# Hybrid decoder trunk: value projection by Strassen blocks with input sums made twice and products in another order

## Chip, cores and metric

One core of one Trainium2 chip runs the whole kernel. The metric is the device time of one execution in microseconds; a profile gives the span from the first to the last instruction, and a little lies around it.

## What is computed

Two residual layers on x of 512 tokens by 2048 columns, float32. The change lies in the second one:

```
def odd_layer(x, ln, w_in, w_out):
    h = rmsnorm(x, ln).astype(x.dtype)
    cq, ck, cv, cg = jnp.split(h @ w_in, 4, axis=-1)      # w_in: 2048 x 8192
    ...
    oc = stick_breaking_attention(heads(cq), heads(ck), heads(cv))
    y = (oc * jax.nn.silu(cg.astype(jnp.float32))).astype(x.dtype) @ w_out
    return x + y
```

The stage in question is `cv`, h (512 x 2048) times the value columns of w_in (2048 x 2048).

## The kernel before

All products run on TensorE (PE) in float32r. Each operand is carried as two parts, hi (a rounded copy made on ScalarE, ACT) and lo (the rest, a subtraction on VectorE, DVE); a product is three matmuls, hi x hi, lo x hi and hi x lo. `split` (line 160) makes the pair. Weights lie in DRAM in the order of use. `plan` lists that order as items, `chunk_pieces` cuts items into transfers, and `pump` fetches and splits them ahead of `take`, three jobs ahead at most, since the pools of hi and lo weights (`wp`) have three buffers. PE's instructions stand in program order. Those of the other engines are ordered by a scheduler by priority, and each engine then works strictly in the order that it was given; a helper `urgent` raises the priority.

The first layer ends with `out_proj`; as each of its 16 column blocks is finished, `finish_even` writes it to DRAM (x1), splits it into h2 and adds its square to a running sum (on GpSimd, POOL). Then comes the value projection (lines 983 to 1018), and after it the q, k and gate projections of 16 heads with attention between them, and the last output projection.

The value projection is 512 x 2048 by 2048 x 2048. `V_ORDER` cuts the 2048 columns into two halves g of 1024 and the 2048 rows into two halves kh, so there are four blocks (g, kh) of 1024 by 1024. Each block takes seven products in place of eight, by Strassen's scheme in Winograd's form. A product is a 256-token half by 512 rows (four chunks of 128) by 512 columns: 24 matmuls of 128 x 512, taken as two jobs of 12. Four products take sums of input quarters (s1 to s4, made by `block_operands` per kh: for each of four pairs of chunks two loads from x1, two scalings on ACT, two sums on POOL, two on DVE and two splits) and four take sums of weight quarters (t1 to t4):

```
G: t3 = 22 - 12 (L220), t1 = 12 - 11 (L221), written over 12
V: t2 = t3 + 11 (L223), written over 11
G: t4 = 21 - t2 (L224), written over 21
```

Here G is POOL and V is DVE. Weight quarters lie in a pool of 19 buffers (x) and, for quarter 11, in three raw buffers of the weights. The blocks come in the order (0,0), (0,1), (1,1), (1,0), so kh changes twice and the input sums are made three times: kh = 0 in the call at n == 11 of `finish_even`, kh = 1 before the second block, kh = 0 again before the fourth. The products come in the order 11, 12, s2, s1, s3, s4, 22, with the weights 11, 21, t2 (in 11), t1 (in 12), t3, 22, t4 (in 21). A result is copied out of PSUM by ACT (L1013) the first time and added by DVE (L1015) afterwards; s2 goes on in the PSUM banks that hold product 11, so it waits for the copy. Finished quarters of a half go to DRAM (`vdr`), from where the heads read them later.

Of the kernel before, what the change touches and what calls it, by code (L numbers as in the profile page):

```python
# [38 lines left out]
def plan():  # L39
# [11 lines left out]
    order += [("wo", "S", 2 * D + 2 * S * g, k) for g, k in V_ORDER]  # L51
# [9 lines left out]
V_ORDER = ((0, 0), (0, 1), (1, 1), (1, 0))  # L61
# [6 lines left out]
def chunk_pieces(item):  # L68
# [9 lines left out]
    if kind == "S":  # L78

        c = 8 * item[3]  # L80
        res = [(c, 2, col, 512), (c + 2, 2, col, 512)] + [(c + i, 1, col, 512) for i in range(4, 8)]
        for i in range(4, 8):
            res += [(c + i, 1, col + 512, 512), (c + i - 4, 1, col + 512, 512)]
        return res
# [14 lines left out]
def trunk(ctx, tc, xt, w, lnT, lbT, gnT, qkn, sink, cs, amask, bmask, eye, cmask, out):  # L99
# [92 lines left out]
    sums = [set() for _ in blocks_at]  # L192
    loaded = set()

    def quarter_load(blk, k):
# [8 lines left out]
        if k < 2:  # L204
            for z in range(2):
                quarters[blk]["11", 2 * k + z] = t[:, z * S:(z + 1) * S]
            quarters[blk]["11 pair", k] = t
        else:
            name = ("21", k - 2) if k < 6 else ("12" if k % 2 else "22", (k - 6) // 2)
            quarters[blk][name] = t  # L210

    def quarter_sums(blk, i, late):

        if (i, late) in sums[blk]:
            return
# [10 lines left out]
    OPERANDS = ("11", "21", "11", "12", "t3", "22", "21")  # L226

    def block_ahead(blk, m):
# [3 lines left out]
        for k in range((0, 1, 2, 4, 6, 10, 14)[min(max(m + 1, 0), 6)]):  # L232
            quarter_load(blk, k)
        for i in range(max(0, min(4, 2 * (m - 3)))):
            quarter_sums(blk, i, False)

    def pump(upto):
        while nxt[0] < min(upto, len(jobs)):
# [3 lines left out]
            if isinstance(j, tuple):  # L242
# [4 lines left out]
                if m in (4, 5):  # L247
                    for i in (2 * m - 8, 2 * m - 7):
                        quarter_sums(blk, i, True)
                hi = wp.tile([P, 2 * S], F32R, tag="hi", name=f"bhi{n}")  # L250
                lo = wp.tile([P, 2 * S], F32R, tag="lo", name=f"blo{n}")
                if OPERANDS[m // 2] == "11":
                    split(quarters[blk]["11 pair", m % 2], hi, lo)
                else:
                    for z in range(2):
                        split(quarters[blk][OPERANDS[m // 2], 2 * (m % 2) + z],
# [582 lines left out]
    def block_operands(kh):  # L839


        res = []
        for i in range(4):
            a, b = U(), U()
            for t, c in ((a, 8 * kh + i), (b, 8 * kh + 4 + i)):
                nc.sync.dma_start(out=t, in_=x1[:, c, :])
                A.activation(out=t, in_=t, func=AF.Copy, scale=ln[:, NC + c:NC + c + 1])  # L847
            a1, a2, b1, b2 = a[:, :256], a[:, 256:], b[:, :256], b[:, 256:]
            G.tensor_tensor(out=b2, in0=a2, in1=b2, op=ALU.add)  # L849
            G.tensor_tensor(out=a2, in0=a1, in1=a2, op=ALU.subtract)  # L850
            V.tensor_tensor(out=a1, in0=b2, in1=a1, op=ALU.subtract)  # L851
            V.tensor_tensor(out=b1, in0=b1, in1=a1, op=ALU.subtract)
            both = []
            for t in (a, b):
                hi, lo = U(F32R), U(F32R)
                split(t, hi, lo)
                both.append((hi, lo))
            res.append(both)
        return res

    def block_op(ops, kh, name, i):
        if name[0] == "s":
            src = ops[i][name in ("s1", "s4")]
# [6 lines left out]
    def finish_even(n, t):  # L870
# [8 lines left out]
        if n == 11:  # L879
            ops0.extend(block_operands(0))  # L880

    ops0 = []
# [101 lines left out]
    PRODUCTS = ("11", "12", "s2", "s1", "s3", "s4", "22")  # L984
    res = None
    for blk, (g, kh) in enumerate(V_ORDER):
        if not blk or V_ORDER[blk - 1][1] != kh:
            ops = ops0 if not blk else block_operands(kh)
        last = blk % 2 == 1
        if not last:  # L990
            res = {}
        pairs = [[bank(pp) for _ in range(2)] for _ in range(2)]
        for n, name in enumerate(PRODUCTS):
            if n in (3,):
                pairs[1] = [bank(pp) for _ in range(2)]
            ps = pairs[n % 2]
            new = n in (0, 1, 3)
            for j in range(2):
                hi, lo = take()
                for i in (2 * j, 2 * j + 1):  # L1000
                    a, b = (x[:, (i % 2) * S:(i % 2 + 1) * S] for x in (hi, lo))
                    xh, xl = block_op(ops, kh, name, i)
                    for t in range(2):
                        k = slice(t * P, (t + 1) * P)
                        mm(ps[t], xh[:, k], a, new and not i, False)
# [109 lines left out]
```

## Time and profile before

| | |
|---|---|
| median of 3 runs | 1864.25 us (1862.08 to 1866.0) |
| the profiled execution | 1865.8 us |
| its span | 1864.0 us |
| PE busy | 1817.4 us (98%) |
| DVE, ACT, POOL busy | 1129.2, 834.5, 193.5 us |
| mean granted clock of TensorE | 0.983 |
| DMA | 208.22 MB, 112 GB/s |

[...] Idle time of an engine that is not the bottleneck costs nothing.

### The profile page before, as it was taken

What the parts mean: (1) busy time and instruction counts of PE and PEld (TensorE: products, weight loads), DVE (VectorE), ACT (ScalarE), POOL (GpSimd) and SP (SyncE); (2) the same over time, 40 slices, a digit from 0 to 9 for tenths busy, and PEclk for the clock granted to TensorE, in tenths of its full rate; (3) what the DMA queues carried; (4) which work ended last, traced back from release to release, by engine and by line L of the source; (5) the groups of instructions that cost most, each with busy time, mean ns of one, the idle gap of its engine ahead of it and who ended that gap; (6) DMA issues with size and microseconds to landing.
All of it is one profiled execution on the core that took longest, in us unless ns stands there. A gap on an engine that the chain in (4) does not pass through costs nothing.

```text
span 1864.0 us, 22949 instructions
## 1 busy us (share of the span) xinstructions
PE 1817.4 (98%) x8706; PEld 1507.6 (81%) x8706; DVE 1129.2 (61%) x1707; ACT 834.5 (45%) x1408; POOL 193.5 (10%) x156
## 2 busy tenths in 40 slices
PE   9999999999999999999879799999999999999999
PEld 6988888888888888887758588888888888888887
DVE  7486777866456676346869646555555456555334
ACT  6454645644344453244545435444545354444221
POOL 4012211200000000125534200000000000000000
PEclk9999999999999999999879799999999999999999
DMA  6222232222221236433343242223223323235424
GB/s 228 91 91 90 80 102 91 91 71 79 83 85 69 80 135 228 174 141 130 103 139 116 79 143 88 88 95 114 85 96 109 101 85 108 96 103 181 163 85 152
DMA packets 79166, 208.22 MB, mean 112 GB/s; under 512 B 9296, under 2 KB 9808, under 8 KB 79056
## 3 DMA queue, kind: packets, MB, share of 16 engines
q1 hardware_dynamic: 76752, 202.57, 32.0%
q10 hardware_dynamic: 2304, 4.20, 0.7%
q8 instruction: 68, 1.11, 0.2%
q14 instruction: 42, 0.34, 0.1%
HBM read 185.76 MB, written 20.97 MB: 111 GB/s over the span
## 4 chain that ended last, share of the span: by engine, by line
PE 91%; DVE 3%; DMA 2%; POOL 1%; ACT 1%; issue 1%; SPq 0%; POOLq 0%; DVEq 0%; ACTq 0%
PE b L158 89%; PE b L944 1%; DMA u<-in_w 1%; DMA u<-x 1%; POOL x L224 1%; DVE blo L162 1%; PE b L603 1%; ACT u L847 0%; ACT u L161 0%; DVE lo L162 0%; DMA raw<-in_w 0%; POOL u L850 0%; POOL u L849 0%; DMA u<-in_xt 0%; ACT bhi L161 0%
## 5 line engine op out<-in xcount | busy, mean ns | idle before, releaser
L158 PE MATMUL b<-u,hi 128*128 128x512 f32 x3584 | 1119.4, 393 | 0.0
L158 PEld LDWEIGHTS b<-u,hi 128*128 128x128 f32 x3584 | 663.2, 188 | 132.4
L158 PE MATMUL b<-u,lo 128*128 128x512 f32 x1792 | 698.8, 390 | 1.0 <-DVE lo L162 1.0
L161 ACT ACTIVATE hi<-raw 128x1024 fp32r<-128x1024 f32 (+2 forms) x266 | 269.9, 1015 | 650.4 <-PE b L158 603.0
L162 DVE TENSOR_TENSOR lo<-raw,hi 128x1024 fp32r<-128x1024 f32 (+2 forms) x266 | 312.4, 1175 | 225.0 <-ACT hi L161 209.9
L158 PEld LDWEIGHTS b<-u,lo 128*128 128x128 f32 x1792 | 336.3, 188 | 72.6 <-DVE lo L162 1.4
L158 PE MATMUL b<-bhi,u 128*128 128x512 f32 x448 | 152.2, 420 | 37.5 <-ACT u L161 24.7
L158 PE MATMUL b<-hi,u 128*128 128x512 f32 (+1 forms) x640 | 185.1, 374 | 2.3 <-ACT u L428 1.7
L158 PEld LDWEIGHTS b<-bhi,u 128*128 128x128 f32 x448 | 90.2, 202 | 65.1 <-ACT u L161 29.9
L158 PEld LDWEIGHTS b<-hi,u 128*128 128x128 f32 x640 | 114.1, 189 | 22.6 <-DVE u L429 2.3
L158 PEld LDWEIGHTS b<-u,u 128*128 128x128 f32 (+2 forms) x928 | 115.6, 176 | 14.9 <-issue 3.5
L158 PE MATMUL b<-u,u 128*128 128x128 f32 (+5 forms) x928 | 126.7, 280 | 0.0
L158 PE MATMUL b<-lo,u 128*128 128x512 f32 (+1 forms) x320 | 118.2, 369 | 0.3 <-DVE lo L162 0.2
L158 PE MATMUL b<-blo,u 128*128 128x512 f32 x224 | 92.7, 414 | 0.2 <-DVE blo L162 0.2
L162 DVE TENSOR_TENSOR blo<-x,bhi 128x512 fp32r<-128x512 f32 x80 | 78.2, 1019 | 20.1 <-ACT bhi L161 20.0
L161 ACT ACTIVATE u<-u 128x512 fp32r<-128x512 f32 (+1 forms) x90 | 54.8, 618 | 66.2 <-DVE u L851 37.8
L373 DVE TENSOR_TENSOR u<-b,bc 128x512 f32<-128x512 f32 x40 | 27.6, 689 | 79.9 <-PE b L158 79.7
L162 DVE TENSOR_TENSOR u<-u,u 128x512 fp32r<-128x512 f32 (+1 forms) x90 | 60.4, 680 | 19.8 <-ACT u L161 19.8
L161 ACT ACTIVATE bhi<-x 128x512 fp32r<-128x512 f32 x80 | 47.1, 623 | 51.5 <-PE b L158 46.7
L158 PEld LDWEIGHTS b<-lo,u 128*128 128x128 f32 x320 | 60.3, 189 | 11.2 <-DVE lo L162 1.1
L220 POOL TENSOR_TENSOR x<-x,x 128x512 f32<-128x512 f32 x16 | 23.3, 1454 | 437.9 <-ACT u L161 402.7
L162 DVE TENSOR_TENSOR x<-x,x 128x512 fp32r<-128x512 f32 (+2 forms) x56 | 32.4, 579 | 58.5 <-ACT x L161 58.5
(174 smaller groups left out, 1655.6 us busy)
## 6 DMA issues: line engine op xcount, KB each, us to landing
raw<-in_w SPq DMA_DIRECT2D x234, 512.0 KB, 3.2
x<-in_w SPq DMA_DIRECT2D x48, 256.0 KB, 2.9
u<-x SPq DMA_DIRECT2D x40, 256.0 KB, 4.2
raw<-in_w SPq DMA_DIRECT2D x24, 384.0 KB, 3.0
ydr<-x SPq DMA_DIRECT2D x32, 256.0 KB, 2.9
u<-ydr SPq DMA_DIRECT2D x32, 256.0 KB, 3.7
u<-in_w SPq DMA_DIRECT2D x16, 256.0 KB, 5.5
u<-in_xt ACTq DMA_DIRECT2D x16, 256.0 KB, 5.0
```

Source lines behind the costliest of these rows:

```text
L158: T.matmul(o, l, r, start=start, stop=stop, skip_group_check=True)
L161: A.activation(out=hi, in_=src, func=AF.Copy)
L162: V.tensor_tensor(out=lo, in0=src, in1=hi.bitcast(F32), op=ALU.subtract)
L220: G.tensor_tensor(out=r["t3", i], in0=r["22", i], in1=r["12", i], op=ALU.subtract)
L224: G.tensor_tensor(out=r["21", i], in0=r["21", i], in1=r["11", i], op=ALU.subtract)
L373: V.tensor_tensor(out=g, in0=ps, in1=bc, op=ALU.mult)
L603: T.transpose(out=pt[:, (2 * i + z) * P:(2 * i + z + 1) * P], in_=probs[p][b][:, z, n * P:(n + 1) * P], identity=ident)
L944: T.transpose(out=o[:, (qb - kb) * P:(qb - kb + 1) * P], in_=zs[qb][:, kb * P:(kb + 1) * P], identity=ident)
```

## The change

Input sums are made twice (the blocks run as (0,0), (1,0), (1,1), (0,1)), the products of even and odd blocks have an order of their own, weight sum t2 moves from DVE to POOL, copies and adds out of PSUM become urgent, the pairs of input sums are called at places of a table, and half g = 0 is written to `vdr` after block 0 and read back during the third block, to be added to in the fourth. In even blocks the product s3 is added to two results (22 and 21), and the product 22 with t4 has banks of its own (from the pool of the attention's banks).

```diff
-V_ORDER = ((0, 0), (0, 1), (1, 1), (1, 0))
+V_ORDER = ((0, 0), (1, 0), (1, 1), (0, 1))
+PRODUCTS = ((("11", "11", 0, 1, ("11",)), ("12", "21", 1, 1, ("11",)), ("22", "t4", 2, 1, ("21",)),
+             ("s2", "t2", 0, 0, ("12",)), ("s1", "t1", 1, 1, ("22",)), ("s3", "t3", 0, 0, ("22", "21")),
+             ("s4", "22", 1, 0, ("12",))),
+            (("11", "11", 0, 1, ("11",)), ("s1", "t1", 1, 1, ("22",)), ("s2", "t2", 0, 0, ("12",)),
+             ("s4", "22", 1, 0, ("12",)), ("s3", "t3", 0, 0, ("22",)), ("12", "21", 1, 1, ("11",)),
+             ("22", "t4", 0, 0, ("21",))))
...
-            V.tensor_tensor(out=r["11", i], in0=r["t3", i], in1=r["11", i], op=ALU.add)
+        elif name == "t2":
+            quarter_sum(blk, "t1", i)
+            r["t2", i] = r["11", i]
+            G.tensor_tensor(out=r["11", i], in0=r["t3", i], in1=r["11", i], op=ALU.add)
...
-        for i in range(max(0, min(4, 2 * (m - 3)))):
-            quarter_sums(blk, i, False)
+        for i in range((0, 0, 0, 2, 4, 4, 4)[m] if blk % 2 else (0, 0, 0, 0, 0, 2, 4)[m]):
+            quarter_sum(blk, "t3", i)
+            quarter_sum(blk, "t1", i)
...
+    def operand_loads(kh, which=range(4)):
+        for i in which:
+            for c in (8 * kh + i, 8 * kh + 4 + i):
+                sources[c] = U()
+                nc.sync.dma_start(out=sources[c], in_=x1[:, c, :])
+    def operand_pair(kh, i):
+        a, b = (sources.pop(c) for c in (8 * kh + i, 8 * kh + 4 + i))
...
-        if n == 11:
-            ops0.extend(block_operands(0))
+        if n == 12:
+            operand_loads(0, (0, 1))
+        if n == 14:
+            operand_pair(0, 0)
...
+    OPERANDS_AT = {(0, 0): ((0, 1),), (0, 1): ((0, 2), (0, 3)),
+                   (1, 5): ((1, 0),), (1, 6): ((1, 1),), (2, 0): ((1, 2),), (2, 1): ((1, 3),)}
+    operand_loads(0, (2, 3))
...
+        for n, (name, _, pair, new, results) in enumerate(PRODUCTS[blk % 2]):
+            if new:
+                banks[pair] = [bank(pa if pair == 2 else pp) for _ in range(2)]
...
+                for to in results:
+                    if (to, t) not in res:
+                        res[to, t] = U()
+                        with urgent():
+                            A.activation(out=res[to, t], in_=ps[t], func=AF.Copy)
+                    else:
+                        with urgent():
+                            V.tensor_tensor(out=res[to, t], in0=ps[t], in1=res[to, t], op=ALU.add)
+                    if to not in left and blk != 1:
+                        tb, cb = t + 2 * (to[0] == "2"), 2 * g + (to[1] == "2")
+                        nc.sync.dma_start(out=vdr[:, tb, cb * S:(cb + 1) * S], in_=res[to, t])
+            if (blk, n) == (1, 4):
+                operand_loads(1)
+            for kh_, i in OPERANDS_AT.get((blk, n), ()):
+                operand_pair(kh_, i)
+            if blk == 2 and n == 4:
+                fetch_half(0)
```

Line numbers move by the change: 162 becomes 170 (lo of a split), 220, 221, 223, 224 become 229, 233, 237, 241 (t3, t1, t2, t4), 849 to 852 become 874 to 877 (the input sums), 1013 and 1015 become 1044 and 1047 (copy and add out of PSUM), 389 becomes 407 (the sum of squares).

How the order moves is shown at three places. Buffers have numbers: raw140 and raw141 hold quarter 11 of block 0, raw154 and raw155 that of block 1, raw168 and raw169 that of block 2; hi and lo weights carry their job's number (bhi140 is the first job of the first block, bhi154 of the second, bhi168 of the third), and x buffers hold other weight quarters.

POOL in the first block, before:

```order
L849 TENSOR_TENSOR u846_7172<-u845_7171,u846_7172 128x256
L850 TENSOR_TENSOR u845_7171<-u845_7171 128x256
L224 TENSOR_TENSOR x866_7292<-x866_7292,raw140_7288 128x512
L224 TENSOR_TENSOR x867_7294<-x867_7294,raw140_7288 128x512
L224 TENSOR_TENSOR x868_7296<-x868_7296,raw141_7290 128x512
L224 TENSOR_TENSOR x869_7298<-x869_7298,raw141_7290 128x512
L849 TENSOR_TENSOR u852_7190<-u851_7189,u852_7190 128x256
L850 TENSOR_TENSOR u851_7189<-u851_7189 128x256
L389 TENSOR_TENSOR u692_5913<-u692_5913,u860_7244 128x512
L389 TENSOR_TENSOR u692_5913<-u692_5913,u864_7284 128x512
L389 TENSOR_TENSOR u692_5913<-u692_5913,u884_7362 128x512
L389 TENSOR_TENSOR u692_5913<-u692_5913,u888_7400 128x512
```

POOL in the first block, with the change, from the first t4 sum on:

```order
L241 TENSOR_TENSOR x846_7228<-x846_7228,raw140_7224 128x512
L241 TENSOR_TENSOR x847_7230<-x847_7230,raw140_7224 128x512
L407 TENSOR_TENSOR u692_5913<-u692_5913,u872_7350 128x512
L241 TENSOR_TENSOR x848_7232<-x848_7232,raw141_7226 128x512
L241 TENSOR_TENSOR x849_7234<-x849_7234,raw141_7226 128x512
L229 TENSOR_TENSOR x908_7597<-x904_7589,x905_7591 128x512
L233 TENSOR_TENSOR x905_7591<-x905_7591,raw154_7543 128x512
L229 TENSOR_TENSOR x909_7600<-x906_7593,x907_7595 128x512
L874 TENSOR_TENSOR u875_7365<-u874_7363,u875_7365 128x256
L233 TENSOR_TENSOR x907_7595<-x907_7595,raw154_7543 128x512
L875 TENSOR_TENSOR u874_7363<-u874_7363 128x256
L874 TENSOR_TENSOR u877_7369<-u876_7367,u877_7369 128x256
```

Before, t4 was the last weight sum of a block and stood here between the input sums of pairs 2 and 3 (u845 and u851); now it is due for the third product, and the input sums of pairs 2 and 3 (u874 and u876) stand behind it and among t3 and t1 of the second block. One more row, the second sum of u876, follows.

DVE in the first block, before:

```order
L162 TENSOR_TENSOR blo143_7436<-x869_7298,bhi143_7435 128x512
L851 TENSOR_TENSOR u851_7189<-u852_7190,u851_7189 128x256
L162 TENSOR_TENSOR blo144_7462<-raw140_7288,bhi144_7461 128x1024
L852 TENSOR_TENSOR u852_7190<-u852_7190,u851_7189 128x256
L162 TENSOR_TENSOR u854_7200<-u851_7189,u853_7199 128x512
L162 TENSOR_TENSOR blo145_7482<-raw141_7290,bhi145_7481 128x1024
L162 TENSOR_TENSOR u856_7204<-u852_7190,u855_7203 128x512
L876 SCALAR_TENSOR_TENSOR u859_7241<-u755_6504,ln_82,u858_7240 128x512
L162 TENSOR_TENSOR blo146_7500<-x871_7302,bhi146_7499 128x512
```

DVE in the first block, with the change:

```order
L1047 TENSOR_TENSOR u880_7409<-b886_7427,u880_7409 128x512
L1047 TENSOR_TENSOR u881_7411<-b887_7428,u881_7411 128x512
L876 TENSOR_TENSOR u874_7363<-u875_7365,u874_7363 128x256
L877 TENSOR_TENSOR u875_7365<-u875_7365,u874_7363 128x256
L876 TENSOR_TENSOR u876_7367<-u877_7369,u876_7367 128x256
L170 TENSOR_TENSOR blo146_7508<-raw140_7224,bhi146_7507 128x1024
L170 TENSOR_TENSOR u889_7484<-u874_7363,u888_7483 128x512
L877 TENSOR_TENSOR u877_7369<-u877_7369,u876_7367 128x256
L170 TENSOR_TENSOR blo147_7524<-raw141_7226,bhi147_7523 128x1024
```

Before, the split of t2 (blo144) stood behind the first DVE sum of pair 3 and was followed by the splits of h2; now (blo146) it stands behind two adds out of PSUM and the DVE sums of pairs 2 and 3.

POOL at the border of the second and third block, with the change:

```order
L874 TENSOR_TENSOR u937_7959<-u936_7957,u937_7959 128x256
L875 TENSOR_TENSOR u936_7957<-u936_7957 128x256
L241 TENSOR_TENSOR x918_7657<-x918_7657,raw154_7543 128x512
L874 TENSOR_TENSOR u939_7963<-u938_7961,u939_7963 128x256
L241 TENSOR_TENSOR x919_7659<-x919_7659,raw154_7543 128x512
L875 TENSOR_TENSOR u938_7961<-u938_7961 128x256
L874 TENSOR_TENSOR u941_7967<-u940_7965,u941_7967 128x256
L875 TENSOR_TENSOR u940_7965<-u940_7965 128x256
L241 TENSOR_TENSOR x920_7661<-x920_7661,raw155_7563 128x512
L229 TENSOR_TENSOR x956_8017<-x952_8009,x953_8011 128x512
L241 TENSOR_TENSOR x921_7663<-x921_7663,raw155_7563 128x512
L233 TENSOR_TENSOR x953_8011<-x953_8011,raw169_7889 128x512
```

All four pairs of kh = 1 (u936 to u943) now stand among t4 of block 1 (x918 to x921) and t3 and t1 of block 2 (x953, x956); twelve more rows follow without anything else between them, among them four of t2 and four of t4 of block 2.

## Rows read from the trace of the kernel before

**Rows 1.** The page of the kernel before, part 2: the clock in 40 slices
```profile
PEclk9999999999999999999879799999999999999999
```

**Rows 2.** Windows view, stage and four stretches: busy us (instructions), clock, DMA
```profile
core 0: us, PE busy (x) PEld busy (x) DVE busy (x) ACT busy (x) POOL busy (x), PEclk, DMA share, GB/s
869.70:1079.90 210.20, 172.57 (x675) 135.06 (x674) 160.67 (x198) 98.33 (x160) 84.68 (x64) 0.85 0.32 107
880.90:900.00 19.10, 8.16 (x25) 6.18 (x23) 14.99 (x18) 9.87 (x18) 9.54 (x7) 0.64 0.27 88
932.00:965.00 33.00, 19.26 (x48) 12.43 (x47) 17.64 (x29) 14.22 (x23) 7.74 (x10) 0.59 0.42 136
965.00:1034.00 69.00, 67.45 (x297) 55.29 (x295) 62.10 (x68) 32.60 (x52) 36.82 (x24) 1.00 0.33 107
1034.00:1062.00 28.00, 16.77 (x42) 11.10 (x43) 15.87 (x27) 12.33 (x22) 4.34 (x6) 0.57 0.32 112
```

**Rows 3.** Timeline of PE: start, us, engine, line, operation [idle before]
```profile
870.41 0.62 PE L158 MATMUL b<-bhi,u 128*128 128x512 f32 x2
871.09 0.62 PE L158 MATMUL b<-bhi,u 128*128 128x512 f32 x2
892.17 1.22 PE L158 MATMUL b<-bhi,u 128*128 128x512 f32 x2 [10.94 <-ACT u L1013]
897.46 0.86 PE L158 MATMUL b<-bhi,u 128*128 128x512 f32 x2
```

**Rows 4.** Groups by line, PE, 869.7 to 1080: xcount, busy, mean ns, idle before
```profile
L158 PE MATMUL b<-bhi,u 128*128 128x512 f32 x448 | 152.2, 420 | 37.5 <-ACT u L161 24.7 <-ACT u L1013 10.9 <-DVE u L162 1.8
```

**Rows 5.** Waits, 869 to 1080: who waited for whom, us in total, times, longest
```profile
PE b L158 <- ACT u L161: 24.7, 8, 5.3
PE b L158 <- ACT u L1013: 10.9, 1, 10.9
DVE u L851 <- POOL u L850: 21.4, 9, 3.9
```

**Rows 6.** Groups by line, DVE, 869.7 to 1080
```profile
L162 DVE TENSOR_TENSOR blo<-x,bhi 128x512 fp32r<-128x512 f32 x80 | 78.2, 1019 | 20.1 <-ACT bhi L161 20.0
L162 DVE TENSOR_TENSOR blo<-raw,bhi 128x1024 fp32r<-128x1024 f32 x15 | 20.4, 1362 | 0.0
L1015 DVE TENSOR_TENSOR u<-b,u 128x512 f32<-128x512 f32 x40 | 26.5, 684 | 4.2 <-PE b L158 4.2
L162 DVE TENSOR_TENSOR u<-u,u 128x512 fp32r<-128x512 f32 x20 | 13.2, 687 | 1.4 <-ACT u L161 1.4
L223 DVE TENSOR_TENSOR raw<-x,raw 128x512 f32<-128x512 f32 x14 | 11.2, 834 | 0.6
L851 DVE TENSOR_TENSOR u<-u,u 128x256 f32<-128x256 f32 x10 | 4.2, 424 | 21.4 <-POOL u L850 21.4
```

**Rows 7.** Groups by line, POOL, 869.7 to 1080
```profile
L224 POOL TENSOR_TENSOR x<-x,raw 128x512 f32<-128x512 f32 x16 | 26.3, 1665 | 27.4 <-DVE blo L162 27.4
L850 POOL TENSOR_TENSOR u<-u 128x256 f32<-128x256 f32 x10 | 7.6, 759 | 0.6
```

**Rows 8.** Timeline, two pieces of DVE and the POOL operations beside the first
```profile
875.47 4.09 DVE L162 TENSOR_TENSOR blo<-x,bhi 128x512 fp32r<-128x512 f32 x3
...
890.55 1.76 DVE L162 TENSOR_TENSOR blo<-x,bhi 128x512 fp32r<-128x512 f32 x1
...
877.33 4.61 POOL L224 TENSOR_TENSOR x<-x,raw 128x512 f32<-128x512 f32 x3 [0.63 <-DVE blo L162]
```

**Rows 9.** Tile and line views, same stretch: shortest, median and longest in ns
```profile
L162 DVE TENSOR_TENSOR blo<-x,bhi x80: 676/692/1791, 874.3 to 1072.6; 128x512 fp32r<-128x512 f32 x80
L162 DVE TENSOR_TENSOR blo<-raw,bhi x15: 1208/1218/2309, 868.9 to 1034.4; 128x1024 fp32r<-128x1024 f32 x15
...
L224 POOL TENSOR_TENSOR x<-x,raw x16: 1272/1682/2264, 875.0 to 1030.0; 128x512 f32<-128x512 f32 x16
```

**Rows 10.** Groups by line, ACT, 840 to 1085
```profile
L847 ACT ACTIVATE u<-u,ln 128x512 f32<-128x512 f32 x24 | 16.7, 714 | 7.7 <-DMA u<-x 7.6
L161 ACT ACTIVATE u<-u 128x512 fp32r<-128x512 f32 x24 | 14.2, 625 | 37.8 <-DVE u L851 37.8
```

More of the change, by code (lines that the diff above doesn't have):

```diff
@@ L50, in plan @@
     order += [("oe", "O", P * n, 1) for n in range(NC)]
-    order += [("wo", "S", 2 * D + 2 * S * g, k) for g, k in V_ORDER]
+    order += [("wo", "S", 2 * D + 2 * S * g, k, b % 2) for b, (g, k) in enumerate(V_ORDER)]
     for h in range(C_HEADS):
@@ L837, in trunk, with block_op @@
     acc2 = U()
[L839 to L861, printed above, removed]
+    ops = {}
+    sources = {}
+    def operand_loads(kh, which=range(4)):
[5 more added lines that the diff above has]
+        a, b = (sources.pop(c) for c in (8 * kh + i, 8 * kh + 4 + i))
+        for t, c in ((a, 8 * kh + i), (b, 8 * kh + 4 + i)):
+            A.activation(out=t, in_=t, func=AF.Copy, scale=ln[:, NC + c:NC + c + 1])
+        a1, a2, b1, b2 = a[:, :256], a[:, 256:], b[:, :256], b[:, 256:]
+        G.tensor_tensor(out=b2, in0=a2, in1=b2, op=ALU.add)
+        G.tensor_tensor(out=a2, in0=a1, in1=a2, op=ALU.subtract)
+        V.tensor_tensor(out=a1, in0=b2, in1=a1, op=ALU.subtract)
+        V.tensor_tensor(out=b1, in0=b1, in1=a1, op=ALU.subtract)
+        ops[kh, i] = []
+        for t in (a, b):
+            hi, lo = U(F32R), U(F32R)
+            split(t, hi, lo)
+            ops[kh, i].append((hi, lo))
+    def block_op(kh, name, i):
         if name[0] == "s":
-            src = ops[i][name in ("s1", "s4")]
+            src = ops[kh, i][name in ("s1", "s4")]
             right = name in ("s3", "s1")
@@ L983, in trunk, with fetch_half @@
     vdr = dr.tile([P, NB, D], F32, tag="vdr", name="vdr")
-    PRODUCTS = ("11", "12", "s2", "s1", "s3", "s4", "22")
-    res = None
-    for blk, (g, kh) in enumerate(V_ORDER):
[L987 to L997, printed above, removed]
+    halves = {0: {}, 1: {}}
+    OPERANDS_AT = {(0, 0): ((0, 1),), (0, 1): ((0, 2), (0, 3)),
+                   (1, 5): ((1, 0),), (1, 6): ((1, 1),), (2, 0): ((1, 2),), (2, 1): ((1, 3),)}
+    operand_loads(0, (2, 3))
+    def fetch_half(g):
+        for key in ("11", "21", "12", "22"):
+            for t in range(2):
+                tb, cb = t + 2 * (key[0] == "2"), 2 * g + (key[1] == "2")
+                halves[g][key, t] = U()
+                nc.sync.dma_start(out=halves[g][key, t], in_=vdr[:, tb, cb * S:(cb + 1) * S])
+    for blk, (g, kh) in enumerate(V_ORDER):
+        res = halves[g]
+        banks = {}
+        for n, (name, _, pair, new, results) in enumerate(PRODUCTS[blk % 2]):
+            if new:
+                banks[pair] = [bank(pa if pair == 2 else pp) for _ in range(2)]
+            ps = banks[pair]
             for j in range(2):
```

58 lines of the change are left out of this document (28 added, 30 removed).

## Prediction

> **What bounds the kernel now.** The page comes first: TensorE (PE) is busy for 98% of the span, and its granted clock is full except in a few slices in the middle [rows 1]. So a time can only be won where PE waits or is slow, and that is one stage, the value projection: its first product starts at 869.7 us and its last ends at 1079.9. The windows view cut at its dips is read next [rows 2]. The unit comes from the timeline of PE [rows 3]: three matmuls every 0.68 us, so 0.2267 us each at the full clock; a job (12 matmuls) is 2.72 us, a product (24) 5.44 us, a block (168) 38.1 us. The stage's 210.2 us hold 675 matmuls, worth 153.0 us, so 57.2 us are lost. Three stretches lose most of it: 880.9 to 900 (25 matmuls, 13.4 us lost), 932 to 965 (48, 22.1 lost), 1034 to 1062 (42, 18.5 lost), 54.0 together; 3.2 are scattered. Between them PE runs at its full rate: 297 matmuls in 69 us.
>
> What is lost has two kinds. PE idles 37.5 us before matmuls that read the sums' splits [rows 4]; the other 19.7 us are matmuls at the lower clock. Rows 3 show one such restart: after the gap of 10.94 us twelve matmuls take 5.29 us (892.17 to 897.46) where 2.72 would do, 2.6 us more. [...] I price each restart at 2.6 us.
>
> The waits by releaser name the cause [rows 5]. 24.7 us of PE's idleness end with ScalarE's split of an input sum, 10.9 with the copy of the first product out of PSUM. The first is the chain of `block_operands`, run at each change of `kh`, four pairs long: scale on ScalarE (ACT), two sums on GpSimd (POOL), two on VectorE (DVE), two splits. The second is the copy that stands on ACT behind that same chain. Everything hangs on three engines' queues, in order.
>
> **The change, step by step.** *Removed: the third round of input sums, and the place of the second.* Four of twelve pairs go: per pair 2 x 0.71 and 2 x 0.63 us of ACT [rows 10], 2 x 0.42 and 2 x 0.69 of DVE [rows 6], 2 x 0.75 of POOL [rows 7]. That is 10.7, 8.9 and 6.0 us off three engines, none of it on the path by itself. On the path is the order: with kh going 0, 0, 1, 1 there is one change, at the border of the second and third block, and five products stand there that use no sum (12 and 22, then 11, 12, 22): 27 us of PE's work as cover. So all 54.0 us of the three dips go; what comes in their place is worked out below.
>
> *Moved: sixteen weight sums from DVE to POOL.* t2 was 14 x 0.834 us on DVE within the stage [rows 6]; on POOL an operation of its size takes 1.67 [rows 7]. POOL gets 16 x 1.67 - 6.0 = 20.7 us more work, DVE some 20 less. *Added: four PSUM adds* of 0.68 us [rows 6] (s3 now feeds two results in each even block), and eight writes and eight reads of 256 KB, since block 0's half goes to DRAM and comes back. I cost these at nothing: the DMA engines are 0.32 busy over the stage [rows 2], the half is read again in the third block for use in the fourth, and each such write waits on SP only for an add that is soon done. If that cover were gone, the loads behind them would be late by the wait; that is part of the upper ends. The copies out of PSUM become urgent, which takes the 10.9 us wait away.
>
> *What is late next, first place: the fourth product of block 0.* It needs t2 and the input sums of pairs 2 and 3. In the change's order POOL makes the four t4 sums first, each after a split on DVE that follows the end of the output projection (869.7 + 0.69 + 0.6, about 871.0), then a square's sum, then four sums of the next block, and among these the four half sums of pairs 2 and 3; DVE's next input sum waits for them, and the split of t2 is queued behind it on DVE. So nine full operations at 1.67 [rows 7] and four half at 0.75: 18.0 us, 889.0. Then three DVE sums (1.3) and the split (1.2): 891.5. PE wants that split two matmuls into the product, 869.7 + 16.3 + 0.5 = 886.5. It is 5.0 us late, with a restart 7.6. Lower end: POOL at its shortest, 1.27 [rows 9], is 887.8 and 1.3 us late. Upper end: what this place costs now, 13.4. I take 7.6, because POOL and DVE both have work all through that stretch, so its mean is the nearer row.
>
> *Second place: the border of blocks 1 and 2.* The pairs of kh = 1 begin on ACT behind the split of job 10 of block 1; its buffer (three deep) is free 7 jobs in, at 19.0 us from the block's start; two splits and two scalings later, at 21.7, POOL starts on 24 operations in a row up to block 2's last t4: 16 full, 8 half, 32.6 us, so to 54.3. DVE has 38 operations there: 22 of 512 columns, 2 of 1024, 6 adds from PSUM, 8 half sums. The price of the 22 is the question. Without POOL at work the median is 0.69 [rows 9], the mean over the stage 1.02 [rows 6], and against an uninterrupted run of POOL three took 4.09 us, 1.36 each [rows 8], while the longest are 1.76 [rows 8]. POOL is uninterrupted here, so 1.36: 29.9 + 2.7 + 4.1 + 3.4 = 40.1 us, from 22.5 to 62.6. PE wants the last split of t4 in block 2 at 19 jobs plus eight matmuls, 53.5. It is 9.1 us late; I count two restarts, since DVE's sums wait for POOL in the middle (a first gap at block 2's first split): 14.3. Lower end: at 1.02 the DVE is done at 55.1, POOL's last sum plus its split at 56.3, 2.8 us late. Upper end: at 1.76, 71.4, 17.9 late, 23.1 with restarts.
>
> *Sum, against the profiled execution's own 1865.8 us (its span is 1864.0, and 1.8 lie around it):* lost after = 7.6 + 14.3 + 3.2 scattered as before = 25.1; gained 57.2 - 25.1 = 32.1. 1865.8 - 32.1 = 1833.7. The median of the runs shown, 1864.25, is 1.55 lower, so **1832**. With both lower ends and nothing scattered 4.1 us are lost: 1811. With both upper ends 39.7: 1847.
>
> [...] The row first: the same subtraction takes DVE 0.68 at the least and 1.79 at the most [rows 9], and POOL 1.27 to 2.26, in stretches where both work; adds that read one operand from PSUM stay at 0.684 [rows 6]. [...]
>
> **The rivals.** [...]
>
> *Both places are covered.* The sums of the input are spread, and if DVE's mean is near 1.02 the border loses 3 us and no restart comes: 1811 to 1820, say 1815. For it: 27 us of PE's work stand at the border. Against: DVE is in order, and its input sums wait for POOL behind the block's own sums.
>
> *Slower: DVE becomes the bound.* If each of the 65 POOL operations holds one DVE operation to 1.76 [rows 8], DVE needs 65 x 1.76 + 29 x 0.69 + 15 x 1.36 + 12 x 0.42 + 44 x 0.68 = 190 us. It also waits for POOL's half sums, 21.4 us in nine waits now [rows 5], and seven of ten pairs stay within the stage: 15 more, 205. PE, fed in short gaps all the way, is at the lower clock as long as now (19.7): 225 in place of 210.2, 1879. It decides from 190.5 us of DVE's work and waits (210.2 - 19.7). For it: between 965 and 1034 DVE is at 90% already [rows 2]. Against: the mean over the 80 splits is 1.02, far from 1.76.
>
> **How the numbers follow.** Forecast 0.50; both covered 0.22; lock binding everywhere 0.18; DVE the bound 0.08; 0.02 for a loss I do not see. A measurement of this kernel can tell some 0.2%, 4 us, from no change. The forecast and the covered case are faster; of the lock's case most is (by 21 us in the middle), a small part lies within 4 us: faster 0.87, within 0.04, slower 0.09. The range takes the forecast's bounds (1811 to 1847), half of the covered case and most of the lock's: 1809 to 1854.
>
> **What would show it.** Right: in the stage's windows no dip of 20 us; three matmuls per 0.68 us through the last block; a gap of about 5 us near the fourth product of block 0, with the releaser DVE's split; a gap or several around the start of block 2, released by DVE's splits, whose mean there is near 1.4; POOL without a pause for some 30 us before. The row "PE waits for ACT's split of an input sum" falls from 24.7 to a few us. Wrong: gaps that end with a DMA (the buffers or SP's queue, which I cost at nothing), gaps in block 3, where I expect none, or a stage as long as 189 us with DVE over 90% busy in all four blocks.

## The result, and the profile after

The changed kernel takes 1842.16 us (median of 4 runs, 1840.83 to 1842.75) against 1863.84 for the kernel before, measured with it: a ratio of 0.9882, 95% interval 0.9865 to 0.9899. The forecast was 1832 in a range from 1809 to 1854, so direction and range held. The gain was 21.7 us where 32 were forecast.

The profiled execution took 1840.83 us. The clock row of the page has no slice below 9 any more [rows 1]:

```profile
PEclk9999999999999999999999999999999999999999
```

The windows view of the stage and of four stretches of it, with the columns of [rows 2]:

```profile
869.50:1055.00 185.50, 162.10 (x675) 127.73 (x675) 162.90 (x175) 89.50 (x145) 100.75 (x68) 0.97 0.40 135
869.50:905.00 35.50, 25.89 (x97) 18.93 (x97) 31.99 (x35) 20.34 (x35) 22.35 (x17) 0.90 0.36 119
905.00:950.00 45.00, 45.00 (x201) 37.24 (x200) 35.29 (x36) 27.18 (x46) 24.24 (x17) 1.00 0.53 177
950.00:1000.00 50.00, 36.20 (x139) 25.98 (x138) 47.16 (x47) 19.00 (x31) 34.74 (x24) 0.97 0.31 105
1000.00:1055.00 55.00, 55.00 (x244) 45.58 (x243) 48.47 (x58) 22.97 (x35) 19.43 (x12) 1.00 0.41 138
```

At 0.2267 us a matmul [rows 3] the 675 matmuls are worth 153.0 us, so 32.5 are lost, after 57.2. The loss stands in two stretches, as forecast: 35.5 - 97 x 0.2267 = 13.5 us around the first block, and 50.0 - 139 x 0.2267 = 18.5 at the border of the second and third. The other 100 us run at the full rate.

PE's waits in the stage (who waited for whom, us in total, times, longest), beside [rows 5]:

```profile
PE b L166 <- DVE blo L170: 22.9, 13, 5.4
```

The 24.7 us for ACT's split of an input sum and the 10.9 for a copy out of PSUM are gone. PE now waits for VectorE's split of a weight, and 0.4 us once for an add. The groups of DVE in the stage, beside [rows 6]:

```profile
L170 DVE TENSOR_TENSOR blo<-x,bhi 128x512 fp32r<-128x512 f32 x80 | 83.7, 1088 | 11.2 <-ACT bhi L169 10.9
L1047 DVE TENSOR_TENSOR u<-b,u 128x512 f32<-128x512 f32 x44 | 28.6, 682 | 2.0 <-PE b L166 1.9
L170 DVE TENSOR_TENSOR u<-u,u 128x512 fp32r<-128x512 f32 x16 | 19.4, 1220 | 0.0
L876 DVE TENSOR_TENSOR u<-u,u 128x256 f32<-128x256 f32 x6 | 5.2, 860 | 4.5 <-POOL u L875 4.5
```

Within the stage DVE lost 14 t2 sums, eight half-size sums and four splits of input sums, and gained no work but four adds, yet its splits take longer: 1088 ns after 1019 for those of weights, 1220 after 687 for those of input sums, 860 after 424 for a half-size sum. The adds that read PSUM stay at 682.

### The profile page after: what moved, and what is told of

It reads as the page before. It is cut to its first block, busy times and chain, and to the rows that moved or that the text cites. A ratio compares the mean times of both kernels' runs of the same rounds, so it can differ in the third digit from the quotient of the medians.

```text
span 1839.0 us, 22928 instructions
## 1 busy us (share of the span) xinstructions
PE 1806.1 (98%) x8706; PEld 1500.0 (82%) x8706; DVE 1131.6 (62%) x1679; ACT 824.5 (45%) x1392; POOL 216.4 (12%) x164
## 4 chain that ended last, share of the span: by engine, by line
PE 91%; DVE 3%; DMA 2%; issue 2%; POOL 1%; ACT 1%; SPq 0%; POOLq 0%; DVEq 0%; ACTq 0%
PE b L166 89%; DVE blo L170 1%; PE b L968 1%; DMA u<-in_w 1%; PE b L621 1%; DVE u L170 1%; DMA raw<-in_w 0%; DVE lo L170 0%; DMA ident<-in_eye 0%; POOL x L241 0%; DVE u L1047 0%; POOL u L407 0%; DMA u<-x 0%; DVE u L876 0%; PE b L552 0%
## 5 line engine op out<-in xcount | busy, mean ns | idle before, releaser
L169 ACT ACTIVATE hi<-raw 128x1024 fp32r<-128x1024 f32 (+2 forms) x266 | 269.9, 1015 | 652.8 <-PE b L166 599.7
L166 PE MATMUL b<-bhi,u 128*128 128x512 f32 x448 | 141.0, 396 | 0.4 <-DVE u L1047 0.4
L166 PEld LDWEIGHTS b<-bhi,u 128*128 128x128 f32 x448 | 85.8, 192 | 18.6 <-ACT bhi L169 0.8
L170 DVE TENSOR_TENSOR blo<-x,bhi 128x512 fp32r<-128x512 f32 x80 | 83.7, 1088 | 11.2 <-ACT bhi L169 10.9
L166 PEld LDWEIGHTS b<-blo,u 128*128 128x128 f32 x224 | 43.0, 192 | 39.1 <-DVE blo L170 30.6
L166 PEld LDWEIGHTS b<-lo,u 128*128 128x128 f32 x320 | 60.3, 189 | 11.2 <-DVE lo L170 1.1
```

Source lines behind the costliest of these rows:

```text
L166: T.matmul(o, l, r, start=start, stop=stop, skip_group_check=True)
L169: A.activation(out=hi, in_=src, func=AF.Copy)
L170: V.tensor_tensor(out=lo, in0=src, in1=hi.bitcast(F32), op=ALU.subtract)
```

## The experiments

All runs of the kernel's parts that keep its result, in one table; e2 and e3, one run each, leave sums unused and stand in the text. "Order" is the product order, "pairs" the place of the input sums' preparation; the last columns say which engine makes the weight sums. Ratios are to the kernel before, which was run beside each on the same chip (three chips in all) and took 1863.8 to 1864.6 in the median.

| run | order | pairs | t2 | t1, t3, t4 | us | ratio, 95% interval |
|---|---|---|---|---|---|---|
| the change | new | spread | POOL | POOL | 1842.16 | 0.9882 (0.9865 to 0.9899) |
| e1 | new | spread | DVE | POOL | 1836.95 | 0.9852 (0.9838 to 0.9867) |
| e12 | new | spread | DVE | DVE | 1822.27 | 0.9771 (0.9754 to 0.9787) |
| e6 | old in even blocks | spread | POOL | POOL | 1836.82 | 0.9850 (0.9835 to 0.9865) |
| e4 | old | spread | POOL | POOL | 1831.94 | 0.9828 (0.9812 to 0.9845) |
| e5 | old | spread | DVE | POOL | 1827.58 | 0.9801 (0.9786 to 0.9816) |
| e10 | old | spread | DVE | DVE | 1824.05 | 0.9783 (0.9767 to 0.9799) |
| e7 | new | lumped | POOL | POOL | 1839.06 | 0.9864 (0.9849 to 0.9878) |
| e9 | old | lumped | POOL | POOL | 1831.81 | 0.9824 (0.9809 to 0.9838) |
| e11, rounds alone | old | lumped | DVE | POOL | 1842.98 | 0.9886 (0.9872 to 0.9901) |
| e8, before + urgent | old | three rounds | DVE | POOL | 1864.94 | 1.0002 (0.9992 to 1.0011) |

### Where the 32.5 us that are left come from: the weight sums

**e1** makes t2 on VectorE again:

```diff
-            G.tensor_tensor(out=r["11", i], in0=r["t3", i], in1=r["11", i], op=ALU.add)
+            V.tensor_tensor(out=r["11", i], in0=r["t3", i], in1=r["11", i], op=ALU.add)
```

> Weight sum t2 goes back to DVE, all else as in the change. Theory (POOL's queue is late, and its operations hold DVE's): the gap of 5.38 us near the fourth product of block 0 shrinks to under 3, the border of blocks 1 and 2 (950 to 1000 us, 18.5 us lost) loses about 6 us less; about 1834 us. Rival (DVE's own work is the bound at the border): DVE gets 16 operations more, 11 to 13 us; slower, about 1848 us.

Measured: 1836.95, 5.2 us faster than the change. The time is near the theory's 1834, its places are not: the longest gap stayed at 5.4 us, and the loss fell by 2.5 us around the first block (108 matmuls from 869.5 to 905 where the change has 97) and by 2.9 at the border (152 from 950 to 1000 for 139), not by 6. The mean of the 80 weight splits fell from 1088 to 998 ns.

**e2** leaves t1, t2 and t4 out (the products then read the unsummed quarters, and the output is another matrix); t3 is made:

```diff
-            G.tensor_tensor(out=r["12", i], in0=r["12", i], in1=r["11", i], op=ALU.subtract)
+            pass
...
-            G.tensor_tensor(out=r["11", i], in0=r["t3", i], in1=r["11", i], op=ALU.add)
+            pass
...
-            G.tensor_tensor(out=r["21", i], in0=r["21", i], in1=r["11", i], op=ALU.subtract)
+            pass
```

> The weight sums t1, t2 and t4 are left out (48 POOL operations; the products take the quarters as loaded); t3 and the input sums stay. Theory: nearly all of the 32.5 us lost in the stage goes, stage about 156 us, whole kernel about 1813 us. Rival (ACT's queue, the PSUM banks or SP's order hold PE at these places): the stage keeps 15 us or more of its loss, 1828 us or more.

Measured: 1813.36 in one run, as the theory said; PE waits 2.6 us in the whole stage. So with these sums gone nothing else in the new stage (DMA, PSUM banks, ACT, half 0's way through DRAM) holds PE for long.

**e3** makes sums of the same size on GpSimd, but into one tile (`bc0`) that nothing else in this stage reads, so no product can wait for them (the products read the unsummed quarters, as in e2):

```diff
-            G.tensor_tensor(out=r["12", i], in0=r["12", i], in1=r["11", i], op=ALU.subtract)
+            G.tensor_tensor(out=bc0, in0=bc0, in1=r["11", i], op=ALU.subtract)
...
-            G.tensor_tensor(out=r["11", i], in0=r["t3", i], in1=r["11", i], op=ALU.add)
+            G.tensor_tensor(out=bc0, in0=r["t3", i], in1=bc0, op=ALU.add)
```

(t4 as t1).

> The sums t1, t2 and t4 are still made on POOL with the same size and two SBUF inputs, but into a buffer that nobody reads; the products take the quarters as loaded. If POOL's operations cost by holding DVE's (contention), the splits of 512 columns keep a mean of 1.05 us or more and the stage is 170 to 182 us (1826 to 1838). If they cost by their data being late, it is like the run without them, about 156 us (1813).

Measured: 1838.69 in one run, just above the range for contention; the mean of the 80 splits is 1050 ns (752 in e2, 1088 in the change). 25 of the 28.8 us between the change and e2 are back although no product reads the sums, so in this run it is not their own lateness that costs. Held splits are one way that is left. There is a second: the unused sums stand on POOL ahead of the input sums. DVE idles for one of these, and then PE, in this run's longest gap:

```profile
873.25 1.47 DVE L876 TENSOR_TENSOR u<-u,u 128x256 f32<-128x256 f32 x1 [9.46 <-POOL u L875]
881.31 0.79 PE L166 MATMUL b<-blo,u 128*128 128x512 f32 x1 [7.86 <-DVE blo L170]
```

How much of the 25 us is held time and how much POOL's queue, e3 does not tell apart.

**e10** and **e12** take GpSimd out of it: all four weight sums on VectorE, with the old product order (e10, on top of e5) and with the change's own (e12). The edit is e1's, for t1, t3 and t4 too.

> The old order with spread pairs and t2 on VectorE, and the other three weight sums (t3, t1, t4; 48 instructions) moved from GpSimd to VectorE as well. Theory (a sum on GpSimd holds VectorE for about as long as VectorE would take for it itself, 1.77 less 0.69 us held against 0.76 us done, so that GpSimd takes nothing off VectorE): 1827.6 within 4. Rival (VectorE gets 48 x 0.76 = 36 us more work in a stage where it is busy already): 1845 or more.

> The changed kernel, its new product order and spread pairs kept, with all four weight sums on VectorE. Theory (the new order costs its 10 us because it lets GpSimd's sums fall due behind the pairs, where they hold VectorE's splits): without GpSimd's sums the two orders are alike, 1824 within 3. Rival (the order costs by itself, since it calls for t4, and in odd blocks for t1, some products earlier, on whichever engine): 1824 plus 10, 1834 within 3.

Measured: 1824.05 and 1822.27, as both theories said, and the two fastest versions that keep the result. e12's stage, its groups on DVE, its waits of PE, and the piece of PE's timeline with its longest gap:

```profile
869.60:1037.70 168.10, 159.44 (x679) 128.55 (x678) 149.83 (x227) 88.60 (x145) 21.16 (x14) 0.98 0.45 149
```

```profile
L170 DVE TENSOR_TENSOR blo<-x,bhi 128x512 fp32r<-128x512 f32 x80 | 52.7, 687 | 8.2 <-ACT bhi L169 7.8
...
L241 DVE TENSOR_TENSOR x<-x,raw 128x512 f32<-128x512 f32 x16 | 11.6, 747 | 0.0
L170 DVE TENSOR_TENSOR u<-u,u 128x512 fp32r<-128x512 f32 x16 | 10.9, 681 | 0.3 <-ACT u L169 0.3
L237 DVE TENSOR_TENSOR raw<-x,raw 128x512 f32<-128x512 f32 x14 | 10.4, 761 | 0.0
L229 DVE TENSOR_TENSOR x<-x,x 128x512 f32<-128x512 f32 x12 | 8.3, 702 | 0.0
L233 DVE TENSOR_TENSOR x<-x,raw 128x512 f32<-128x512 f32 x12 | 8.1, 685 | 0.1
```

```profile
PE b L166 <- DVE blo L170: 7.2, 5, 4.7
PE b L166 <- ACT bhi L169: 1.3, 2, 0.7
```

```profile
892.41 0.59 PE L166 MATMUL b<-blo,u 128*128 128x512 f32 x1 [4.66 <-DVE blo L170]
```

VectorE takes on 11.6 + 10.4 + 8.3 + 8.1 = 38.4 us of sums and is still busy for less: 149.8 us after 162.9. Two groups of splits alone give back 83.7 - 52.7 = 31.0 and 19.4 - 10.9 = 8.5 us, together 39.5; all of VectorE's work apart from the sums takes 111.4 us in place of 162.9. Handing these sums to GpSimd takes nothing off VectorE here; it costs more held time than the work itself. The move also empties POOL's queue ahead of the input sums, so the 19.9 us between the change and e12 are not divided between the two ways. The loss in the stage is 168.1 - 153.0 = 15.1 us in place of 32.5.

### The product order

**e4** keeps the block order, the spreading and the engines, but takes the old product order in all blocks, with t4 made next to t2:

```diff
+PRODUCTS = ((("11", "11", 0, 1, ("11",)), ("12", "21", 1, 1, ("11",)), ("s2", "t2", 0, 0, ("12",)),
+             ("s1", "t1", 1, 1, ("22",)), ("s3", "t3", 0, 0, ("22",)), ("s4", "22", 1, 0, ("12",)),
+             ("22", "t4", 0, 0, ("21",))),) * 2
...
-                        quarter_sum(blk, name, 2 * (m % 2) + z)
+                        quarter_sum(blk, "t4" if name == "t2" else name, 2 * (m % 2) + z)
```

(with the order of loads and sums ahead as in even blocks, and half 1's loads one product later).

> Products in the order of the kernel before (11, 12, s2, s1, s3, s4, 22) in every block, with the blocks, the two rounds of input sums, t2 on POOL and the places of the pairs as in the change. Theory: the change of kh is covered by three products (16 us) in place of five and t2 and the pairs are due earlier in each block; the border loses 10 us more, 1850 to 1858 us. Rival (only the number of rounds counts): within 4 us of 1842.

Measured: 1831.94, and both expectations fell: the new order costs 10.2 us. e4's windows of the first block and of the border, with the columns of [rows 2]:

```profile
870.00:900.00 30.00, 22.82 (x80) 16.34 (x79) 29.05 (x32) 18.46 (x32) 17.61 (x12) 0.89 0.43 138
950.00:990.00 40.00, 32.69 (x128) 24.00 (x127) 37.81 (x42) 21.14 (x34) 23.23 (x19) 0.96 0.37 120
```

They lose 11.9 and 11.0 us, where the change loses 13.5 and 18.5: most of the difference is at the border.

**e6** puts back the even blocks' order alone.

```diff
-PRODUCTS = ((("11", "11", 0, 1, ("11",)), ("12", "21", 1, 1, ("11",)), ("22", "t4", 2, 1, ("21",)),
-             ("s2", "t2", 0, 0, ("12",)), ("s1", "t1", 1, 1, ("22",)), ("s3", "t3", 0, 0, ("22", "21")),
-             ("s4", "22", 1, 0, ("12",))),
+PRODUCTS = ((("11", "11", 0, 1, ("11",)), ("12", "21", 1, 1, ("11",)), ("s2", "t2", 0, 0, ("12",)),
+             ("s1", "t1", 1, 1, ("22",)), ("s3", "t3", 0, 0, ("22",)), ("s4", "22", 1, 0, ("12",)),
+             ("22", "t4", 0, 0, ("21",))),
```

> Only the even blocks' order is put back (t4's product last instead of third); the odd blocks keep the new order, t4 is made on demand. Theory (the new order costs because t4, on top of t2, is due at the third product of an even block, right behind the pair sums, where GpSimd's sums hold VectorE's): nearly all of the 10 us that the old order in all blocks gave, 1832 to 1835. Rival (it is the odd blocks' order, whose sums t3 and t1 are needed at the second product): no gain, 1842 within 3.

Measured: 1836.82, half of the 10 us. Neither expectation held: the early t4 of even blocks is one half; the other half goes with the odd blocks' order or with t4 made on demand, which e6 does not tell apart.

**e5** is e4 with e1's edit.

> The order of products of before kept in the changed kernel, and in addition t2 made on VectorE again. Theory (the product order and t2's engine cost for different reasons, so that their gains add): 1831.9 (old order alone) less the 5.2 us that t2 on VectorE alone gave, about 1827 (1824 to 1829). Rival (both remove the same wait of TensorE for the low part of a weight split): no further gain, 1832 within 2.

Measured: 1827.58, within the theory's range and 4.4 us below e4; the two gains add. And e12 against e10 settles what the order costs by itself: with the sums on VectorE the new order is 1.8 us below the old one, so it costs nothing. Its 10 us need GpSimd's sums.

### Where the gain came from

**e7** takes the change and lumps the pairs again; **e9** does the same to e4, the fourth corner.

```diff
-    OPERANDS_AT = {(0, 0): ((0, 1),), (0, 1): ((0, 2), (0, 3)),
-                   (1, 5): ((1, 0),), (1, 6): ((1, 1),), (2, 0): ((1, 2),), (2, 1): ((1, 3),)}
-    operand_loads(0, (2, 3))
+    OPERANDS_AT = {(1, 6): ((1, 0), (1, 1), (1, 2), (1, 3))}
...
-        if n == 12:
-            operand_loads(0, (0, 1))
-        if n == 14:
-            operand_pair(0, 0)
+        if n == 11:
+            operand_loads(0)
+            for i in range(4):
+                operand_pair(0, i)
```

> The changed kernel with the preparation of the input sums lumped again: the four pairs of half 0 at tile 11 of the output projection, the four pairs of half 1 together behind block 1's last product. Theory (spreading is a part of the gain; VectorE's work on the four pairs, 4 x (0.89 + 0.70 + 2 x 1.22) = 16 us under GpSimd's sums, then stands in one piece ahead of the weight splits, of which the products without sums cover about half): slower than the changed kernel by 5 to 12, 1847 to 1854. Rival (the products without input sums at the border are cover enough, and where the pairs stand is indifferent): 1842 within 3.

> The fourth corner of order by preparation: the old product order in all blocks and all pairs lumped (half 0 at tile 11 of the output projection, half 1 behind block 1), with the two rounds of sums and t2 on GpSimd as in the change. Theory (each of the two, the products without sums at the border and the spreading, is cover enough by itself, so one may be missing, but not both: the old dip of 22 us at the second round comes back): 1850 to 1856. Rival (neither is what took the dips away; two rounds in place of three and nothing else did, and the parts add): 1839.1 (lumped, new order) less 10.2 (the order), 1829 within 4.

Measured: 1839.06 and 1831.81; both theories fell. Spreading gains nothing with either order (3.1 us against it in one, with executions that overlap, and 0.1 in the other), and without both the spreading and the cover of the new order the dip of 22 us does not come back. The time of e9 is that of its rival, but e11 below shows that two rounds alone do not give it.

**e8** is the kernel before with one part of the change, the urgent copies and adds:

```diff
-                    A.activation(out=res[to, t], in_=ps[t], func=AF.Copy)
+                    with urgent():
+                        A.activation(out=res[to, t], in_=ps[t], func=AF.Copy)
```

(and the add below it).

> The kernel before with one part of the change alone: the copies and adds out of PSUM are put ahead of other ready work on ScalarE and VectorE. Theory (the 10.94 us wait of TensorE for a copy out of PSUM goes, with the low clock behind it, and nothing takes its place): 1850 to 1854. Rival (TensorE then waits as long for the input sums, whose splits the copies were queued behind): 1861 to 1865.

Measured: 1864.94, no gain, in the rival's range. PE's longest wait in its stage still ends with the copy, as before:

```profile
PE b L158 <- ACT u L1014: 10.9, 1, 10.9
```

**e11** is the kernel before with the block order alone changed: against e9, t2 is on VectorE, the copies are not urgent, and each pair's loads stand right ahead of it:

```diff
-            if (blk, n) == (1, 5):
-                operand_loads(1)
...
+        operand_loads(kh, (i,))
         a, b = (sources.pop(c) for c in (8 * kh + i, 8 * kh + 4 + i))
```

> The kernel before with one part of the change alone, the one that no run has yet taken away: the block order (0,0), (1,0), (1,1), (0,1), so that the input sums are made twice and not three times, and half 0's results through DRAM. All else as before: product order, t2 on VectorE, each pair's two loads issued right ahead of it, the four pairs in one piece, copies out of PSUM not urgent. Theory (this part is nearly all of the gain): 1831.8 (old order, lumped) less 5 for t2 on VectorE, 1827 within 3. Rival (it is the loads of the input sums issued ahead of the pairs, which the lumped version still had; in the kernel before POOL waited 7.6 and 6.7 us in the second round for scaled tiles whose loads were issued late): the second round's dip of about 22 us comes back and 1845 to 1852 results.

Measured: 1842.98, 16 us above the theory and 2 below the rival's range, and the border's dip came back. The gain is 21.4 us, most of it the third dip (18.5); the other two are nearly as before. Its windows around them:

```profile
876.00:900.00 24.00, 12.89 (x50) 9.92 (x49) 18.68 (x22) 13.72 (x24) 13.62 (x10) 0.79 0.36 120
965.00:1000.00 35.00, 19.13 (x58) 12.81 (x57) 18.87 (x31) 13.50 (x23) 9.35 (x11) 0.71 0.53 174
```

They lose 12.7 and 21.9 us; before it was 13.4 and 22.1. The trace shows what the second waits for. The rows of SP that issue transfers, then one row of POOL and one of PE:

```profile
955.08 0.90 SPq L860 DMA_DIRECT2D u<-x  x2
971.00 0.33 SPq L207 DMA_DIRECT2D raw<-in_w  x1
971.43 0.85 SPq L860 DMA_DIRECT2D u<-x  x2
```

```profile
976.79 0.72 POOL L870 TENSOR_TENSOR u<-u,u 128x256 f32<-128x256 f32 x1 [7.45 <-ACT u L868]
```

```profile
979.49 1.52 PE L163 MATMUL b<-bhi,u 128*128 128x512 f32 x2 [6.14 <-ACT u L166]
```

The waits view of SP from 930 to 1000 names what held it:

```profile
SPq L207 <- DVE blo L167: 44.9, 19, 15.0
```

A weight load (L207) stood on SP for 15.0 us until VectorE's split freed its buffer. The second pair's two loads (L860) were queued behind it; ACT, POOL, DVE and at last PE wait for them in turn. The kernel before has the same picture: SP idle from 919.5 until a `raw` load at 934.50, and the pair's loads at 934.95. In e9 the last five of these loads go out in a row, ahead of the `raw` load:

```profile
947.32 2.34 SPq L860 DMA_DIRECT2D u<-x  x5
951.71 7.42 SPq L207 DMA_DIRECT2D x<-in_w  x3
980.41 0.33 SPq L207 DMA_DIRECT2D raw<-in_w  x1
```

From e11 to e9 the time falls by 11.2 us, nearly all of it at the border: e9 loses 11.5 us from 945 to 1000 (192 matmuls) where e11 loses 21.9, and 11.4 around the first block for 12.7. If t2 on GpSimd costs the 4.4 us there that e4 and e5 differ by, loads ahead and urgent copies are worth 11.2 + 4.4 = 15.6 together. Urgent copies alone gave nothing in e8; the early loads without them were not tried, so that the loads are what counts is read from the traces.

So the change adds up as: two rounds in place of three -21.4; loads ahead with urgent copies -15.6; t2 on GpSimd +4.4 (e4 against e5); spreading -0.1 to +3.1; the new order, under GpSimd's sums, +10.2; with the spreading at 0 that is -22.4, where -21.7 was measured. The terms are steps from run to run (kernel before, e11, e9, e4, the change), so the sum must come out near and is no proof of the single terms.

## Why the prediction was right, and where it was off

**The bound and the places held.** PE's long waits are in this stage alone, in block 0 up to its fourth product and around the start of block 2, for DVE's splits; no gap ends with a DMA, and block 3 runs at the full rate (clock 1.00 from 1000 to 1055). On the profiled executions the gain was 1865.8 - 1840.8 = 25.0 us where 32.1 were forecast, and the terms of the loss account for it: the first place 13.5 us for 7.6, the border 18.5 for 14.3, scattered 0.5 for 3.2; together 7.4 more.

**First place: the step left out what stands on POOL ahead of t4, and POOL began 5.9 us later.** The step let POOL's t4 sums begin at about 871.0, behind DVE's add at the end of the output projection. The timeline of DVE and POOL there:

```profile
871.74 3.36 DVE L170 TENSOR_TENSOR u<-u,u 128x512 fp32r<-128x512 f32 x2
875.02 0.68 DVE L850 TENSOR_TENSOR u<-b,u 128x512 f32<-128x512 f32 x1
```

```profile
871.12 3.44 POOL L237 TENSOR_TENSOR raw<-x,raw 128x512 f32<-128x512 f32 x2 [2.73 <-DVE blo L170]
874.51 1.73 POOL L407 TENSOR_TENSOR u<-u,u 128x512 f32<-128x512 f32 x1
876.87 3.38 POOL L241 TENSOR_TENSOR x<-x,raw 128x512 f32<-128x512 f32 x2 [0.63 <-DVE blo L170]
...
895.28 0.79 POOL L875 TENSOR_TENSOR u<-u 128x256 f32<-128x256 f32 x1
```

Two t2 sums and a square stand on POOL ahead of t4, and while the t2 sums ran DVE's two splits took 3.36 us instead of 1.4; the add came at 875.02, t4 began at 876.87, and the chain ended at 896.1. The t2 sums are there because the change itself moved them. The chain's own length was nearly right (19.2 us for 18.0). PE's timeline shows four small gaps of 0.50 to 1.42 us, which the step did not have, before the long one. In all PE is 11.4 us late at this split (897.88 for 886.5), not 5.0:

```profile
897.88 0.79 PE L166 MATMUL b<-blo,u 128*128 128x512 f32 x1 [5.38 <-DVE blo L170]
```

**Border: the price of the splits came out, POOL's run without a pause did not.** The step took 1.36 us for each of 22 splits, since three took 4.09 against "an uninterrupted run of POOL" [rows 8]. That row has a pause of POOL inside it (0.63 us), so it was misread. The groups of DVE from 953 to 991 hold 22 such splits, and they took 30.3 us for the 29.9 forecast:

```profile
L170 DVE TENSOR_TENSOR blo<-x,bhi 128x512 fp32r<-128x512 f32 x14 | 18.3, 1342 | 0.0
L170 DVE TENSOR_TENSOR u<-u,u 128x512 fp32r<-128x512 f32 x8 | 12.0, 1501 | 0.0
```

The price was right by luck: POOL paused here too, although the prediction named its run without a pause as a sign of being right. Where it has sum after sum, a split takes 1.77 us, the step's upper end. First POOL, then DVE:

```profile
944.31 0.74 POOL L874 TENSOR_TENSOR u<-u,u 128x256 f32<-128x256 f32 x1 [3.15 <-ACT u L872]
...
969.10 7.05 POOL L237 TENSOR_TENSOR raw<-x,raw 128x512 f32<-128x512 f32 x4 [3.63 <-DVE blo L170]
976.11 3.40 POOL L241 TENSOR_TENSOR x<-x,raw 128x512 f32<-128x512 f32 x2
980.20 3.30 POOL L241 TENSOR_TENSOR x<-x,raw 128x512 f32<-128x512 f32 x2 [0.69 <-DVE blo L170]
```

```profile
947.02 1.52 DVE L876 TENSOR_TENSOR u<-u,u 128x256 f32<-128x256 f32 x1
...
971.52 1.78 DVE L170 TENSOR_TENSOR blo<-x,bhi 128x512 fp32r<-128x512 f32 x1
973.22 1.78 DVE L170 TENSOR_TENSOR u<-u,u 128x512 fp32r<-128x512 f32 x1
...
985.89 3.48 DVE L170 TENSOR_TENSOR blo<-x,bhi 128x512 fp32r<-128x512 f32 x2
```

POOL's 24 sums run from 944.31 to 983.50, 39.2 us for the 32.6 forecast: 33.2 us of work, as priced, and 6.0 us of waiting, all for DVE's splits. The two engines wait for each other (DVE 1.89 us at 951.31 for POOL's sum), which the step had in one direction only. DVE's first input sum starts at 947.02, some 26 us after the start of block 1 (about 921 by the count of matmuls) where 22.5 was forecast, and its last t4 split ends at 989.4, some 68 for 62.6. PE is thus about 15 us late there for 9.1. Behind it t2's splits come late once more, and the clock falls after that gap, to 0.70 from 995 to 1000:

```profile
993.45 0.50 PE L166 MATMUL b<-blo,u 128*128 128x512 f32 x1 [2.36 <-DVE blo L170]
```

Of the two restarts counted, this one came.

**"So all 54.0 us of the three dips go": not by the reason given.** By place, the third dip went with its round (18.5 us), the second fell from 22.1 to 18.5, the scattered loss from 3.2 to 0.5, and the first stayed: 13.4 before, 13.5 after, with another releaser. The step put the border down to the five products without sums. e4 and e9 have two fewer there and lose less (11.0 and 11.5 us); e11 has as many as e9 and loses 21.9. The traces of e11 and e9 put that down to the loads that no longer stand behind a waiting weight load. The prediction named three queues, ACT, POOL and DVE; the fourth, SP's, where this chain began, was costed at nothing.

**"The copies out of PSUM become urgent, which takes the 10.9 us wait away": not by itself.** In e8 the copies are urgent and the wait is still 10.9 us; in e11, without urgent copies, it is too. In the change it is gone, with the loads ahead as well; no run shows which of the parts is needed.

**"DVE some 20 less": never came.** The sums went, and held splits took their place: DVE was busy for 162.9 us after 160.7.

**The rivals.** The case that the chances call the lock (VectorE's and GpSimd's work adding up over the whole stage, to 189 us and so 1843) came closest in number, but not as described: from 905 to 950 and from 1000 to 1055 PE ran at the full rate with DVE busy for 83.8 and POOL for 43.7 of 100 us, and the loss was at two places. That the work of the two adds up was the author's premise; no run shows it. What the runs show is longer instructions: in the change a split of 512 columns took 1.77 us where POOL made sum after sum (971.52 to 978.3), in e12, without POOL's weight sums, 687 ns in the mean; the adds that take their other input from PSUM stayed at 682. GpSimd's weight sums cost more than the 0.18 suggests: without them the same order takes 1822.27 us, 19.9 less, of which the share of the longer splits is not known. That both places are covered (1815) was refuted by the two gaps; that DVE becomes the bound (1879) by DVE's 162.9 us in a stage of 185.5.

## What to carry to other kernels

Before work is given to GpSimd to relieve VectorE, set what VectorE would take for it (here 38.4 us) against how much longer VectorE's own instructions take beside it (here 39.5 on two groups of splits alone): if both are alike, keep the work on VectorE. Where a chain begins with a load, look in the issuing queue at what stands ahead of it; in e11 one that waited 15.0 us for a buffer held those behind it, and issuing the others earlier, with urgent copies, was worth some 16 us where a new order of products gave back 10. A change of many parts is read by its corners: here one part gained 21 us, two together 16, one nothing, and two gave back 15.

The version to keep is e12, the change with all weight sums on VectorE: 1822.27 us, 42 below the kernel before and 20 below the change.

## What the hardware showed that was not expected

- Small instructions took longer too: half-size sums on DVE took 0.86 us in the mean after 0.42 in the kernel before, and two casts of 128 x 128 to bf16, with one input each, took 2.55 us in the change (882.42, while POOL made t4 sums) and 0.35 in the kernel before (896.80, with POOL idle).
- In e12 one square sum on POOL is shown with 9.70 us (876.74), the one before it with 1.59 (870.76), while DVE ran instruction after instruction, those of 128 x 512 with two inputs at 0.68 each. Whether POOL waited for DVE there was not tested.
- In the change, gaps of PE of up to 2.58 us, one every 2 to 9 us, left the granted clock at 1.00 from 950 to 990; it fell after the gap of 5.38 us, to 0.56 from 897.88 to 903, and about 1 us behind one of 2.36 (993.45), with the 18 matmuls of 995 to 1000 at 0.70.
